# Long convolution with its matrices loaded and three tiles summed by taps; global attention in packed halves

## The chip, the core and the metric

The kernel runs on one core of a Trainium2 chip. Its time is the device time of one execution in microseconds (us). TensorE (PE, with PEld for its weight loads) multiplies into PSUM; VectorE (DVE), ScalarE (ACT) and GpSimd (POOL) work on SBUF and PSUM; SyncE (SP) and ScalarE issue DMAs.

## The reference

A network of two blocks, batch 1, 512 positions, width 1024, all float32. The first block has two layers, each a mixer (global attention, pooling, neighbourhood attention, gates) and a gated MLP with a convolution of 3 taps. The second has a conformer module, a convolution FFN, dilated attention and another FFN. The change touches two parts:

```python
def global_axial_attention(q, k, v, gq, gk):      # both layers: 8 query heads, 2 key heads, 64 wide
    q = rope_2d(rmsnorm(q, gq)) * 64 ** -0.5; k = rope_2d(rmsnorm(k, gk))
    s = jnp.einsum('bqkgd,bskd->bkgqs', qi, k)
    p = jax.nn.softmax(s, axis=-1)
    return jnp.einsum('bkgqs,bskd->bqkgd', p, v)

def conformer_conv_module(h, w_in, b_in, dw, dw_b, ln_g, ln_b, w_out, b_out):   # once
    u = h @ w_in + b_in
    u = u[..., :1024] * jax.nn.sigmoid(u[..., 1024:])
    u = causal_dwconv(u, dw, dw_b)                # 31 taps, each channel by itself
    u = jax.nn.silu(layer_norm(u, ln_g, ln_b))
    return u @ w_out + b_out
```

## The kernel before

Weights come as units of eight 128x128 tiles, 512 KB, in the order in which they are used: SP loads one (`raw`, 3 buffers), ACT rounds it to a high half (L295), DVE subtracts for the low half (L296), 4 buffers `w`. A product in float32 accuracy is three matmuls into one PSUM bank, high by high, high by low, low by high (`mm3`, L325 to L327). Activations stand transposed, features on partitions, 512 positions along the free side.

Every engine takes its instructions in an order fixed when the program is built. The stages are Python generators, called lanes: a lane yields an estimate of how long its next step has to wait, every matmul adds its estimate to a common clock (`spend`), and lanes that are due are written out between the matmuls of the main loop (`tick`). A scheduler then orders the instructions under the limits of the buffers.

**Global attention** (`axial_inputs`, `axial_lane`). Two query heads share the 128 partitions of a tile `qh`/`ql` (the pair is i, the head in it e). The keys of head e stand in 64 partitions of `kh`/`kl` [:, e], with zeros in the other 64, so scores for 128 queries are three 512-column matmuls (L862 to L864). After softmax (DVE maximum, ACT exponential, POOL scaling) the probabilities are transposed and split into `ph`/`pl`, and for each of four key blocks three 256-column matmuls (L890, L893, L894) add into `po`; values `vh`/`vl` carry zeros for the other head, and `po` of a pair collects four units. Two lanes run beside the gate and branch matmuls of `branch`.

**Long convolution** (`conv_inputs`). For each of 8 feature tiles j two projections are computed, ACT evacuates them (`ca` L1234, `cgs` L1239) and DVE multiplies them into `cu` with positions split by their remainder mod 4 (L1241). Sixteen small DMAs (L1249) bring that into `cup`, where a partition is a pair of remainder and channel. POOL builds matrices `cw` from the taps (L1224), and 36 plain float32 matmuls of 128 columns a tile do the 31 taps (L1264; the profile shows each as two records). DVE adds the bias (`vc`, L1274), PE transposes (`ctp`, L1281), ACT copies to `vt`, DVE takes statistics (L1288). When all eight tiles are in, statistics are joined (L1291), `vt` is normalised, and PE transposes it back (`ltp`, L1185) for the closing product. The first six projections (tiles 0 to 2) come out of the head, which runs while the norm of the stage ahead is still coming in.

Of the kernel before, what the change touches and what calls it, by code (L numbers as in the profile page):

```python
# [21 lines left out]
F32 = mybir.dt.float32  # L22
# [6 lines left out]
P = 128  # L29
# [14 lines left out]
CONV_M, CONV_PAD = 9, 8  # L44
AX_LANES, AX_SOFTMAX, AX_NEXT, AX_PROB = 2, 5.5, 2.0, 1.7
# [111 lines left out]
_vec("cm_b_in", 16)  # L157
for _n in ("cm_ln_g", "cm_ln_b", "kv_norm_g"):
    _vec(_n, 8)
# [11 lines left out]
def constants():  # L171
# [29 lines left out]
    c["same"] = np.tile(np.eye(32, dtype=np.float32), (4, 1))  # L201
# [25 lines left out]
class Kernel:  # L227
# [534 lines left out]
    def axial_inputs(self, l):  # L762
# [64 lines left out]
        return jobs, (kh, kl, vh, vl, qh, ql, rq), done  # L827
# [21 lines left out]
    def axial_lane(self, units, st, tiles, y):  # L849

        nc = self.nc
        kh, kl, vh, vl, qh, ql, rq = tiles
        yh, yl = y
        while units:
            i, u, e = units.popleft()
# [3 lines left out]
            for t in (2 * u, 2 * u + 1):  # L859
                cols = slice(t * P, (t + 1) * P)  # L860
                ps = self.psum("a", "sc")
                nc.tensor.matmul(ps, qh[:, i, cols], kh[:, e], start=True, stop=False)  # L862
                nc.tensor.matmul(ps, qh[:, i, cols], kl[:, e], start=False, stop=False)
                nc.tensor.matmul(ps, ql[:, i, cols], kh[:, e], start=False, stop=True)  # L864
                self.spend(0.65)
# [15 lines left out]
            if i not in st:  # L881
                st[i] = self.psum("b", "po")
                st[i, "n"] = 0
            po = st[i]
            cols = slice(2 * u * P, (2 * u + 2) * P)
            for k in range(4):
# [8 lines left out]
            self.spend(1.3)  # L895
            st[i, "n"] += 1
            if st[i, "n"] == 4:
                self.split_out(yh[:, i], yl[:, i], po)
# [303 lines left out]
    def conv_inputs(self):  # L1202

        nc, cv = self.nc, self.cv
        taps = cv.tile([P, 32, CONV_M, 4], F32, tag="taps", name="taps")
        nc.sync.dma_start(
            taps, self.t["cm_taps"].rearrange("p (g m q) -> p g m q", m=CONV_M, q=4)
        )  # L1210
        same = cv.tile([P, 32], F32, tag="same", name="same")
        nc.sync.dma_start(same, self.t["same"])
# [5 lines left out]
        held, phased, mats = [], {}, {}  # L1218
# [34 lines left out]

        def conv():
            for j in range(KD):
# [17 lines left out]
                vc = cv.tile([P, 4, P], F32, tag="vc", name="vc", bufs=2)  # L1273
# [37 lines left out]
        matrices(0)  # L1311
        matrices(1)
# [286 lines left out]
def arrange(inputs):  # L1599
# [44 lines left out]
    put("cm_b_in", a["cm_b_in_2"][0])  # L1644

# [3 lines left out]
    got["cm_taps"] = np.ascontiguousarray(  # L1649
# [32 lines left out]
```

## Time and profile before

| | us |
|---|---|
| median of 3 runs (3252.04 to 3722.86) | 3252.92 |
| the profiled execution | 3250.97 |
| its span, first to last instruction | 3249.2 |
| PE busy in it | 3157.3 |
| DVE busy in it | 1783.0 |
| ACT busy in it | 1329.3 |
| POOL busy in it | 493.7 |

The profile is of one execution. A matmul's record is longer than the time it takes from its neighbours, since matmuls overlap: what one costs in a dense row is the distance from its start to the next one's. A bracket at the end of a line is the idle time ahead of the instruction and what ended it. PEclk is the granted TensorE clock as a share of full speed.

### The profile page before, as it was taken

How to read it: one execution, taken by the hardware profiler on the slowest of the kernel's cores; microseconds unless marked ns; L12 is line 12 of the kernel's file. 1: busy time of each engine (PE TensorE's matmuls, PEld its weight loads, DVE VectorE, ACT ScalarE, POOL GpSimd, SP SyncE). 2: the span in 40 equal slices, each digit the busy share in tenths (PEclk: the TensorE clock that was granted, in tenths of full speed). 3: DMA queues.
4: the chain of work that ended last, by engine and by line, in shares of the span. 5: the costliest groups of instructions: out<-in, count | busy, mean ns of one | idle time of the engine just before them, and what ended most of it. 6: DMA issues, size and time to landing. Idle time of an engine off the chain costs nothing.

```text
span 3249.2 us, 41363 instructions
## 1 busy us (share of the span) xinstructions
PE 3157.3 (97%) x16172; PEld 2664.2 (82%) x16172; DVE 1783.0 (55%) x3187; ACT 1329.3 (41%) x2160; POOL 493.7 (15%) x448
## 2 busy tenths in 40 slices
PE   8999999999999999999999989999899999999998
PEld 7887888888888788888879868888788888888886
DVE  6668446456675753645465356446634454464555
ACT  5456334334444643434343154334333333353332
POOL 0113110000111322000005410000433334100001
PEclk9999999999999999999999989999999999999999
DMA  3112232222221222232232222222222222222221
GB/s 141 59 61 74 98 111 79 97 100 94 91 69 53 77 87 101 84 104 96 95 108 77 67 80 71 98 97 104 84 72 79 77 78 79 79 85 98 97 98 72
DMA packets 86403, 281.80 MB, mean 87 GB/s; under 512 B 11584, under 2 KB 17984, under 8 KB 86208
## 3 DMA queue, kind: packets, MB, share of 16 engines
q1 hardware_dynamic: 85632, 278.10, 24.7%
q8 instruction: 128, 2.10, 0.3%
q10 hardware_dynamic: 576, 1.05, 0.1%
q14 instruction: 67, 0.55, 0.1%
HBM read 274.91 MB, written 2.10 MB: 85 GB/s over the span
## 4 chain that ended last, share of the span: by engine, by line
PE 87%; DVE 8%; ACT 4%; issue 1%; DMA 0%; POOL 0%; SPq 0%; DVEq 0%; ACTq 0%; POOLq 0%
PE mm L327 18%; PE mm L326 18%; PE mm L325 18%; PE mm L511 6%; PE mm L512 6%; PE mm L513 6%; PE conv L1264 2%; ACT junk L382 2%; PE z L327 1%; PE z L326 1%; PE z L325 1%; DVE w L296 1%; PE htp L444 1%; PE pt L875 1%; PE dpo L1398 1%
## 5 line engine op out<-in xcount | busy, mean ns | idle before, releaser
L325 PE MATMUL mm<-hh,w 128*128 128x512 f32 (+1 forms) x2720 | 1052.7, 387 | 0.0
L326 PE MATMUL mm<-hl,w 128*128 128x512 f32 (+1 forms) x2720 | 1035.2, 381 | 0.0
L327 PE MATMUL mm<-hh,w 128*128 128x512 f32 (+1 forms) x2720 | 1035.0, 381 | 0.0
L296 DVE TENSOR_TENSOR w<-raw,w 128x1024 fp32r<-128x1024 f32 x436 | 567.8, 1302 | 465.7 <-ACT w L295 461.0
L327 PEld LDWEIGHTS mm<-hh,w 128*128 128x128 f32 x2720 | 511.8, 188 | 96.5 <-issue 1.2
L326 PEld LDWEIGHTS mm<-hl,w 128*128 128x128 f32 x2720 | 512.6, 188 | 90.4 <-issue 2.4
L325 PEld LDWEIGHTS mm<-hh,w 128*128 128x128 f32 x2720 | 512.3, 188 | 90.2 <-issue 1.9
L295 ACT ACTIVATE w<-raw 128x1024 fp32r<-128x1024 f32 x436 | 459.0, 1053 | 247.7 <-PE mm L513 187.0
L403 POOL TENSOR_TENSOR y<-y,row 128x512 f32<-128x512 f32 x40 | 54.3, 1389 | 1311.1 <-ACT junk L382 1311.1
L625 DVE SCALAR_TENSOR_TENSOR cg<-mm,vecs,cg 128x511 f32<-128x511 f32 (+1 forms) x176 | 131.9, 749 | 212.8 <-ACT cg L618 209.9
L292 POOL TENSOR_TENSOR raw<-raw,vecs 128x1024 f32<-128x1024 f32 x72 | 145.5, 2021 | 562.2 <-DMA raw<-in_wall 558.2
L512 PE MATMUL mm<-w,ah 128*128 128x512 f32 x576 | 226.5, 393 | 0.0
L511 PE MATMUL mm<-w,ah 128*128 128x512 f32 x576 | 225.7, 392 | 0.0
L513 PE MATMUL mm<-w,al 128*128 128x512 f32 x576 | 225.7, 392 | 0.0
L625 DVE SCALAR_TENSOR_TENSOR cv<-mm,vecs,cv 128x511 f32<-128x511 f32 (+1 forms) x176 | 131.9, 750 | 100.2 <-ACT cv L618 97.3
L618 ACT ACTIVATE cg<-mm,vecs 128x512 f32<-128x512 f32 x88 | 68.7, 781 | 286.3 <-PE mm L327 286.1
L326 PE MATMUL mm<-hl,keep 128*128 128x256 f32 x512 | 143.4, 282 | 7.0 <-DVE hl L675 6.9
L327 PE MATMUL mm<-hh,keep 128*128 128x256 f32 x512 | 142.9, 281 | 0.1
L325 PE MATMUL mm<-hh,keep 128*128 128x256 f32 x512 | 142.1, 284 | 0.2 <-ACT hh L674 0.2
L511 PEld LDWEIGHTS mm<-w,ah 128*128 128x128 f32 x576 | 109.1, 189 | 23.5 <-issue 0.8
L513 PEld LDWEIGHTS mm<-w,al 128*128 128x128 f32 x576 | 109.1, 189 | 22.6
L512 PEld LDWEIGHTS mm<-w,ah 128*128 128x128 f32 x576 | 109.1, 189 | 22.4
(287 smaller groups left out, 4552.8 us busy)
## 6 DMA issues: line engine op xcount, KB each, us to landing
raw<-in_wall SPq DMA_DIRECT2D x500, 512.0 KB, 3.2
row<-in_rows SPq DMA_DIRECT2D x9, 512.0 KB, 4.1
x<-in_x SPq DMA_DIRECT2D x4, 512.0 KB, 6.1
bt<-in_rpb SPq DMA_DIRECT2D x16, 128.0 KB, 2.1
cup<-cu SPq DMA_DIRECT2D x128, 16.0 KB, 1.8
out<-x SPq DMA_DIRECT2D x4, 256.0 KB, 2.1
out<-x ACTq DMA_DIRECT2D x4, 256.0 KB, 2.1
taps<-in_cm_taps SPq DMA_DIRECT2D x1, 576.0 KB, 4.9
```

Source lines behind the costliest of these rows:

```text
L292: nc.gpsimd.tensor_tensor(rows, rows, g[:, k0 : k0 + n, None].to_broadcast(list(rows.shape)), op=OP.mult)
L295: nc.scalar.activation(hi, raw, AF.Copy)
L296: nc.vector.tensor_tensor(lo, raw, hi.bitcast(F32), op=OP.subtract)
L325: nc.tensor.matmul(ps, wh, xh, start=first and i == 0, stop=False, **check)
L326: nc.tensor.matmul(ps, wh, xl, start=False, stop=False, **check)
L327: nc.tensor.matmul(ps, wl, xh, start=False, stop=stop, **check)
L382: self.nc.scalar.activation(junk, x, AF.Square, accum_out=total)
L511: nc.tensor.matmul(ps, xh, wh, start=first, stop=False)
L512: nc.tensor.matmul(ps, xh, wl, start=False, stop=False)
L513: nc.tensor.matmul(ps, xl, wh, start=False, stop=last)
L618: nc.scalar.activation(o, ps, AF.Identity, scale=self.vec(taps + str(k0), f), bias=self.vec(cb, f))
L625: nc.vector.scalar_tensor_tensor(o[:, to], ps[:, of], self.vec(taps + str(k), f), o[:, to], op0=OP.mult, op1=OP.add,)
```

## The change

**Attention.** The tile `q` [:, i, e] now holds head e alone: its high half in the 64 partitions of that head and its low half in the other 64. Keys stand in both halves of `kh` and `kl`, so one matmul with `kh` gives high by high and low by high together, and scores take two matmuls. `v` is packed in the same way, so `po` has two parts in its two halves, added at the end by ACT and DVE, once for each head rather than each pair. The zero fills go, the units run head by head.

**Convolution.** The matrices `cw` are laid out in DRAM and loaded by DMAs that ACT issues, 590 KB each, four a tile. Feature tiles 0 to 2 don't go to the matrices: they stay in the order of positions with 30 zeros ahead, ACT does tap 0 and the bias, DVE does 30 multiply-adds (`scalar_tensor_tensor`), and PE transposes the result as before. The taps stand in `vecs`, which grows from 868 to 1124 columns.

```diff
+CONV_DVE, CONV_TAP = 3, 1.0
...
+_vec("cm_dw_b", 8)
+for _k in range(31):
+    _vec(f"cm_dw{_k}", 8)
...
-        vh = self.ap.tile([P, 4, 2, P], F32R, tag="vh", name="vh")
-        vl = self.ap.tile([P, 4, 2, P], F32R, tag="vl", name="vl")
-        qh = self.ap.tile([P, 4, S], F32R, tag="qh", name="qh")
-        ql = self.ap.tile([P, 4, S], F32R, tag="ql", name="ql")
+        v = self.ap.tile([P, 4, 2, P], F32R, tag="v", name="v")
+        q = self.ap.tile([P, 4, 2, S], F32R, tag="q", name="q")
...
-        zero = self.rp.tile([P, S], F32, tag="wide", name="zero")
-        nc.gpsimd.memset(zero, 0.0)
-        none = zero[:, :256].rearrange("p (i d) -> p i d", i=4)
-        for v in (vh, vl):
-            nc.scalar.activation(v[:, :, 0, 64:], none, AF.Copy)
-            nc.scalar.activation(v[:, :, 1, :64], none, AF.Copy)
-        for k in (kh, kl):
-            nc.scalar.activation(k[64:, 0], zero[64:], AF.Copy)
-            nc.scalar.activation(k[:64, 1], zero[:64], AF.Copy)
...
-            for e, r in ((0, slice(0, 64)), (1, slice(64, P))):
+            for e in range(2):
+                r, o = ends[e], ends[1 - e]
                 nc.scalar.activation(kh[r, e], qg[r], AF.Copy)
-                nc.vector.tensor_tensor(kl[r, e], qg[r], kh[r, e].bitcast(F32), op=OP.subtract)
+                nc.scalar.activation(kh[o, e], qg[r], AF.Copy)
+                for to in (r, o):
+                    nc.vector.tensor_tensor(kl[to, e], qg[r], kh[r, e].bitcast(F32), op=OP.subtract)
...
-            self.split_out(vh[:, :, 0, :64], vl[:, :, 0, :64], pt[:, :, :64])
-            self.split_out(vh[:, :, 1, 64:], vl[:, :, 1, 64:], pt[:, :, 64:])
+            self.split_out(v[:, :, 0, :64], v[:, :, 0, 64:], pt[:, :, :64])
+            self.split_out(v[:, :, 1, 64:], v[:, :, 1, :64], pt[:, :, 64:])
...
-            self.split_out(qh[:, i], ql[:, i], qg)
+            for e in range(2):
+                r, o = ends[e], ends[1 - e]
+                nc.scalar.activation(q[r, i, e], qg[r], AF.Copy)
+                nc.vector.tensor_tensor(q[o, i, e], qg[r], q[r, i, e].bitcast(F32), op=OP.subtract)
...
-                nc.tensor.matmul(ps, qh[:, i, cols], kh[:, e], start=True, stop=False)
-                nc.tensor.matmul(ps, qh[:, i, cols], kl[:, e], start=False, stop=False)
-                nc.tensor.matmul(ps, ql[:, i, cols], kh[:, e], start=False, stop=True)
+                nc.tensor.matmul(ps, q[:, i, e, cols], kh[:, e], start=True, stop=False)
+                nc.tensor.matmul(ps, q[:, i, e, cols], kl[:, e], start=False, stop=True)
...
-                    po[:, cols], vh[:, k, e], a, start=st[i, "n"] == 0 and k == 0, stop=False, **check
-                )
-                nc.tensor.matmul(po[:, cols], vh[:, k, e], b, start=False, stop=False, **check)
-                nc.tensor.matmul(po[:, cols], vl[:, k, e], a, start=False, stop=k == 3, **check)
+                    po[:, cols], v[:, k, e], a, start=st[i, e, "n"] == 0 and k == 0, stop=False, **check
+                )
+                nc.tensor.matmul(po[:, cols], v[:, k, e], b, start=False, stop=k == 3, **check)
...
-                self.split_out(yh[:, i], yl[:, i], po)
+                r, o = (slice(0, 64), slice(64, P)) if e == 0 else (slice(64, P), slice(0, 64))
+                t = self.xp.tile([P, S], F32, tag="pot", name="pot", bufs=2)
+                nc.scalar.activation(t[r], po[o], AF.Copy)
+                nc.vector.tensor_tensor(t[r], t[r], po[r], op=OP.add)
+                self.split_out(yh[r, i], yl[r, i], t[r])
...
-                    units = deque((i, u, e) for i in range(4) for u in range(2) for e in range(2))
+                    units = deque((i, e, u) for i in range(4) for e in range(2) for u in range(2))
...
             w = self.cf.tile([P, 4, CONV_M, 4, 32], F32, tag="cw", name="cw", bufs=2)
             for i in range(4):
-                nc.gpsimd.tensor_tensor(
-                    w[:, i],
-                    taps[:, 4 * j + i, :, :, None].to_broadcast([P, CONV_M, 4, 32]),
-                    same[:, None, None, :].to_broadcast([P, CONV_M, 4, 32]),
-                    op=OP.mult,
+                nc.scalar.dma_start(
+                    w[:, i],
+                    self.t["cm_mats"][4 * (j - CONV_DVE) + i].rearrange(
+                        "p (m a b) -> p m a b", m=CONV_M, b=32
+                    ),
                 )
...
+            if j < CONV_DVE:
+                u = cv.tile([P, 30 + S], F32, tag="cw30", name="cw30", bufs=2)
+                nc.gpsimd.memset(u[:, :30], 0.0)
+                nc.vector.tensor_tensor(u[:, 30:], held.pop(), g, op=OP.mult)
+                plain[j] = u
+                return
...
+        def tap_sums():
+            for j in range(CONV_DVE):
+                while j not in plain:
+                    yield 0.5
+                yield 1.4
+                acc = cv.tile([P, S], F32, tag="cacc", name="cacc", bufs=2)
+                nc.scalar.activation(
+                    acc, plain[j][:, :S], AF.Identity, scale=self.vec("cm_dw0", j),
+                    bias=self.vec("cm_dw_b", j),
+                )
+                vc = cv.tile([P, 4, P], F32, tag="vc", name="vc", bufs=3)
+                for k in range(1, 31):
+                    yield CONV_TAP
+                    to, u, of = acc, plain[j][:, k : k + S], acc
+                    if k == 30:
+                        to = vc.rearrange("p q s -> p s q")
+                        u, of = (a.rearrange("p (s q) -> p s q", q=4) for a in (u, acc))
+                    nc.vector.scalar_tensor_tensor(
+                        to, u, self.vec(f"cm_dw{k}", j), of, op0=OP.mult, op1=OP.add
+                    )
...
         def conv():
-            for j in range(KD):
+            for j in range(CONV_DVE, KD):
...
+            while len(summed) < CONV_DVE:
+                yield 0.3
...
-        matrices(0)
-        matrices(1)
+        matrices(CONV_DVE)
+        matrices(CONV_DVE + 1)
+        self.spawn(tap_sums())
         self.spawn(conv())
```

Two places of the order that every engine follows are shown. The first is DVE's queue at the start of the convolution, from the first gated tile on: `w_` are low halves of weights, `cacc<-cw_14415` and `cacc<-cw_14422` taps of tile 0 and tile 1, `cu` and `vc` as above. Before:

```order
L1241 TENSOR_TENSOR cu<-ca,cgs 128x128x4 x2
L296 TENSOR_TENSOR w_14750<-raw_14608,w_14750 128x1024
L296 TENSOR_TENSOR w_14802<-raw_14748,w_14802 128x1024
L1241 TENSOR_TENSOR cu<-ca,cgs 128x128x4
L1274 TENSOR_TENSOR vc<-conv,cbias 128x512
```

And now:

```order
L1243 TENSOR_TENSOR cw_14415<-ca,cgs 128x512
L1243 TENSOR_TENSOR cw_14422<-ca,cgs 128x512
L1279 SCALAR_TENSOR_TENSOR cacc<-cw_14415,vecs,cacc 128x512 x2
L300 TENSOR_TENSOR w_14472<-raw_14433,w_14472 128x1024
L1279 SCALAR_TENSOR_TENSOR cacc<-cw_14415,vecs,cacc 128x512
L300 TENSOR_TENSOR w_14528<-raw_14470,w_14528 128x1024
L1279 SCALAR_TENSOR_TENSOR cacc<-cw_14415,vecs,cacc 128x512
L1279 SCALAR_TENSOR_TENSOR cacc<-cw_14422,vecs,cacc 128x512
L1279 SCALAR_TENSOR_TENSOR cacc<-cw_14415,vecs,cacc 128x512
L300 TENSOR_TENSOR w_14564<-raw_14526,w_14564 128x1024
```

The weights' low halves now stand between taps, and the taps of tiles 0 and 1 alternate; those of tile 2 come later, one behind the other, when tile 0 has given its buffer back. PE, which before went to the convolution of tile 0 after 7 matmuls of the fourth tile's projection, now does 99 matmuls first, and then the matrices of tile 3.

The second place is DVE's queue at the end of the convolution, up to the joining of the statistics (BN_AGGR). Before:

```order
L296 TENSOR_TENSOR w_15598<-raw_15552,w_15598 128x1024
L1274 TENSOR_TENSOR vc<-conv,cbias 128x512
L1288 BN_STATS stats<-ctp 128x6 x4
L1274 TENSOR_TENSOR vc<-conv,cbias 128x512
L1288 BN_STATS stats<-ctp 128x6 x4
L1291 BN_AGGR lmv<-stats 128x2 x4
```

And now:

```order
L300 TENSOR_TENSOR w_15390<-raw_15344,w_15390 128x1024
L1279 SCALAR_TENSOR_TENSOR cacc<-cw_14429,vecs,cacc 128x512 x6
L1313 TENSOR_TENSOR vc<-conv,cbias 128x512
L1327 BN_STATS stats<-ctp 128x6 x4
L1313 TENSOR_TENSOR vc<-conv,cbias 128x512
L1279 SCALAR_TENSOR_TENSOR vc<-cw_14422,vecs,cacc 128x128x4
L1279 SCALAR_TENSOR_TENSOR vc<-cw_14429,vecs,cacc 128x128x4
L1327 BN_STATS stats<-ctp 128x6 x4
L1290 BN_STATS stats<-ctp 128x6 x8
L1332 BN_AGGR lmv<-stats 128x2 x4
```

The last taps of tiles 1 and 2 stand behind the bias of the last matrix tile, and eight more statistics follow.

## Rows read from the trace of the kernel before

**Rows 1.** The page, part 1: busy us of each engine, share, instructions.

```profile
PE 3157.3 (97%) x16172; PEld 2664.2 (82%) x16172; DVE 1783.0 (55%) x3187; ACT 1329.3 (41%) x2160; POOL 493.7 (15%) x448
```

**Rows 2.** The page, part 4: the chain that ended last, by engine.

```profile
PE 87%; DVE 8%; ACT 4%; issue 1%; DMA 0%; POOL 0%; SPq 0%; DVEq 0%; ACTq 0%; POOLq 0%
```

**Rows 3.** Busy us by stretch: PE, PEld, DVE, ACT, POOL, PEclk, DMA share, GB/s.

```profile
50.00:90.00 40.00, 39.45 (x196) 30.30 (x195) 34.97 (x96) 20.65 (x33) 6.33 (x4) 1.00 0.23 80
91.00:223.00 132.00, 130.96 (x726) 111.55 (x725) 76.87 (x165) 63.62 (x122) 24.37 (x33) 1.00 0.15 53
1752.70:1877.50 124.80, 123.20 (x850) 112.55 (x848) 43.62 (x54) 22.18 (x29) 67.07 (x35) 1.00 0.21 67
1877.50:1893.60 16.10, 4.82 (x21) 3.67 (x21) 10.43 (x28) 11.17 (x12) 0.00 (x0) 0.55 0.41 130
```

**Rows 4.** PE's timeline in layer 0's attention: start us, us, engine, line, operation.

```profile
109.41 0.39 PE L864 MATMUL sc<-kh,ql 128*128 128x512 f32 x1
109.64 0.28 PE L890 MATMUL po<-ph,vh 128*128 128x256 f32 x1
...
109.99 0.28 PE L890 MATMUL po<-ph,vh 128*128 128x256 f32 x1
```

**Rows 5.** Groups by line, both layers: count | busy us, mean ns | idle before.

```profile
L894 PE MATMUL po<-ph,vl 128*128 128x256 f32 x128 | 36.1, 282 | 0.0
L864 PE MATMUL sc<-kh,ql 128*128 128x512 f32 x64 | 25.2, 394 | 0.0
...
L1050 DVE TENSOR_TENSOR wot<-wot,wpo 64x512 f32<-64x512 f32 x16 | 11.0, 686 | 6.7 <-ACT wot L1049 6.2
```

**Rows 6.** PE's timeline: the third score of layer 0.

```profile
94.61 0.50 PE L862 MATMUL sc<-kh,qh 128*128 128x512 f32 x1 [0.88 <-DVE rrs L757]
```

**Rows 7.** PE's timeline at the end of the convolution.

```profile
1867.83 8.20 PE L1264 MATMUL conv<-cup,cw 128*128 128x128 f32 x72
1876.82 0.66 PE L1281 MATMUL ctp<-ident,vc 128*128 128x128 f32 x4 [0.78 <-DVE vc L1274]
1886.61 2.98 PE L1185 MATMUL ltp<-ident,vt 128*128 128x128 f32 x12 [9.13 <-DVE vt L1306]
...
1894.57 0.63 PE L511 MATMUL mm<-w,ch 128*128 128x512 f32 x1
1895.00 0.63 PE L512 MATMUL mm<-w,ch 128*128 128x512 f32 x1
```

**Rows 8.** DVE's timeline in an FFN: dependent multiply-adds, then a weight's low half.

```profile
575.25 1.54 DVE L625 SCALAR_TENSOR_TENSOR cg<-mm,vecs,cg 128x511 f32<-128x511 f32 x2 [2.77 <-ACT cg L618]
576.70 1.22 DVE L296 TENSOR_TENSOR w<-raw,w 128x1024 fp32r<-128x1024 f32 x1
577.83 0.69 DVE L642 TENSOR_TENSOR cg<-cg,cv 128x512 f32<-128x512 f32 x1
```

**Rows 9.** DVE's timeline near the end: independent multiply-adds from SBUF.

```profile
3243.23 2.74 DVE L409 SCALAR_TENSOR_TENSOR x<-y,rst,x 128x512 f32<-128x512 f32 x4
```

**Rows 10.** DVE's timeline in the convolution.

```profile
1859.33 1.07 DVE L1241 TENSOR_TENSOR cu<-ca,cgs 128x512 f32<-128x512 f32 x1 [1.89 <-ACT cgs L1239]
...
1876.07 0.69 DVE L1274 TENSOR_TENSOR vc<-conv,cbias 128x512 f32<-128x512 f32 x1 [6.52 <-PE conv L1264]
1878.14 0.89 DVE L1288 BATCH_NORM_STATS2 stats<-ctp 128x6 f32<-128x128 f32 x4 [1.38 <-ACT vt L1284]
1878.95 1.04 DVE L1291 BATCH_NORM_AGGREGATE lmv<-stats 128x2 f32<-128x48 f32 x4
```

**Rows 11.** ACT's timeline: the gate of tile 2.

```profile
1752.94 0.69 ACT L1239 ACTIVATE cgs<-mm,vecs 128x512 f32<-128x512 f32 x1 [1.30 <-PE mm L327]
```

**Rows 12.** SP's queue: the sixteen DMAs of one tile.

```profile
1860.56 10.01 SPq L1249 DMA_DIRECT2D cup<-cu  x16
```

**Rows 13.** DMA issues by tile: KB each, median us to landing.

```profile
raw<-in_wall SPq DMA_DIRECT2D x500, 512.0 KB, 3.2
```

**Rows 14.** DVE's timeline at the start.

```profile
7.76 0.26 DVE L1550 TENSOR_SCALAR hb<-vecs 128x24 f32<-128x24 f32 x2 [6.89 <-DMA vecs<-in_vecs]
```

More of the change, by code (lines that the diff above doesn't have):

```diff
@@ L200, in constants @@
     c["nmask"] = np.stack([edge, inside], 1).astype(np.float32)
-    c["same"] = np.tile(np.eye(32, dtype=np.float32), (4, 1))
     q = np.arange(P)[:, None]
@@ L766, in axial_inputs @@
         kl = self.ap.tile([P, 2, S], F32R, tag="kl", name="kl")
-        vh = self.ap.tile([P, 4, 2, P], F32R, tag="vh", name="vh")
-        vl = self.ap.tile([P, 4, 2, P], F32R, tag="vl", name="vl")
-        qh = self.ap.tile([P, 4, S], F32R, tag="qh", name="qh")
-        ql = self.ap.tile([P, 4, S], F32R, tag="ql", name="ql")
+        v = self.ap.tile([P, 4, 2, P], F32R, tag="v", name="v")
+        q = self.ap.tile([P, 4, 2, S], F32R, tag="q", name="q")
         rq = self.ap.tile([P, 4, 8], F32, tag="rq", name="rq")
-        zero = self.rp.tile([P, S], F32, tag="wide", name="zero")
-        nc.gpsimd.memset(zero, 0.0)
-        none = zero[:, :256].rearrange("p (i d) -> p i d", i=4)
-        for v in (vh, vl):
-            nc.scalar.activation(v[:, :, 0, 64:], none, AF.Copy)
-            nc.scalar.activation(v[:, :, 1, :64], none, AF.Copy)
-        for k in (kh, kl):
-            nc.scalar.activation(k[64:, 0], zero[64:], AF.Copy)
-            nc.scalar.activation(k[:64, 1], zero[:64], AF.Copy)
+        ends = (slice(0, 64), slice(64, P))
         done = [False] * 4
@@ L826, in axial_inputs @@
             jobs.append((gemm_tiles("w_in", l, [T_Q + i], range(KD)), lambda ps, i=i: on_q(ps, i)))
-        return jobs, (kh, kl, vh, vl, qh, ql, rq), done
+        return jobs, (kh, kl, v, q, rq), done
     def softmax_rows(self, ps, scale_col, scale, pmat, mx=None):
@@ L851, in axial_lane @@
         nc = self.nc
-        kh, kl, vh, vl, qh, ql, rq = tiles
+        kh, kl, v, q, rq = tiles
         yh, yl = y
         while units:
-            i, u, e = units.popleft()
+            i, e, u = units.popleft()
             while not st["ready"][i]:
@@ L880, in axial_lane @@
                 yield AX_PROB
[L881 to L884, printed above, removed]
+            if (i, e) not in st:
+                st[i, e] = self.psum("b", "po")
+                st[i, e, "n"] = 0
+            po = st[i, e]
             cols = slice(2 * u * P, (2 * u + 2) * P)
@@ L890, in axial_lane @@
                 nc.tensor.matmul(
-                    po[:, cols], vh[:, k, e], a, start=st[i, "n"] == 0 and k == 0, stop=False, **check
+                    po[:, cols], v[:, k, e], a, start=st[i, e, "n"] == 0 and k == 0, stop=False, **check
                 )
-                nc.tensor.matmul(po[:, cols], vh[:, k, e], b, start=False, stop=False, **check)
-                nc.tensor.matmul(po[:, cols], vl[:, k, e], a, start=False, stop=k == 3, **check)
-            self.spend(1.3)
-            st[i, "n"] += 1
-            if st[i, "n"] == 4:
-                self.split_out(yh[:, i], yl[:, i], po)
+                nc.tensor.matmul(po[:, cols], v[:, k, e], b, start=False, stop=k == 3, **check)
+            self.spend(0.95)
+            st[i, e, "n"] += 1
+            if st[i, e, "n"] == 2:
+                r, o = (slice(0, 64), slice(64, P)) if e == 0 else (slice(64, P), slice(0, 64))
[3 more added lines that the diff above has]
+                self.split_out(yh[r, i], yl[r, i], t[r])
     def window_inputs(self, l):
@@ L1206, in conv_inputs @@
         nc, cv = self.nc, self.cv
-        taps = cv.tile([P, 32, CONV_M, 4], F32, tag="taps", name="taps")
-        nc.sync.dma_start(
-            taps, self.t["cm_taps"].rearrange("p (g m q) -> p g m q", m=CONV_M, q=4)
-        )
-        same = cv.tile([P, 32], F32, tag="same", name="same")
-        nc.sync.dma_start(same, self.t["same"])
         bias = cv.tile([P, 32], F32, tag="cbias", name="cbias")
@@ L1217, in conv_inputs @@
         stats = cv.tile([P, 4, KD, 6], F32, tag="stats", name="stats")
-        held, phased, mats = [], {}, {}
+        held, phased, mats, plain = [], {}, {}, {}
         def matrices(j):
@@ L1252, in on_g @@
             phased[j] = up
+        summed = []
+        def tap_sums():
[18 more added lines that the diff above has]
+                    )
+                yield 1.0
+                pt = self.psum("a", "ctp")
+                for q in range(4):
+                    nc.tensor.transpose(pt[:, q * P : (q + 1) * P], vc[:, q], self.ident)
+                self.spend(0.45)
+                by = pt.rearrange("s (q c) -> s q c", q=4)
+                nc.scalar.activation(vt[:, :, j * P : (j + 1) * P], by, AF.Copy)
+                for q in range(4):
+                    nc.vector.bn_stats(stats[:, q, j], by[:, q])
+                summed.append(j)
         def conv():
-            for j in range(KD):
+            for j in range(CONV_DVE, KD):
                 while min(j + 1, KD - 1) not in phased:
@@ L1272, in conv @@
                     matrices(j + 2)
-                vc = cv.tile([P, 4, P], F32, tag="vc", name="vc", bufs=2)
+                vc = cv.tile([P, 4, P], F32, tag="vc", name="vc", bufs=3)
                 nc.vector.tensor_tensor(
@@ L1644, in arrange @@
     put("cm_b_in", a["cm_b_in_2"][0])
+    put("cm_dw_b", a["cm_dw_b_2"][0])
+    for k in range(31):
+        put(f"cm_dw{k}", a["cm_dw_2"][0, k])
     dw = np.pad(a["cm_dw_2"][0][::-1], ((3, 6), (0, 0))).reshape(40, 32, 32)
     q, m, p = np.ogrid[:4, :CONV_M, :4]
-    got["cm_taps"] = np.ascontiguousarray(
-        dw[4 * m + p - q + 3].transpose(0, 4, 3, 1, 2).reshape(P, 32 * CONV_M * 4)
-    )
+    taps = dw[4 * m + p - q + 3].transpose(0, 4, 3, 1, 2)[:, :, 4 * CONV_DVE :]
+    mats = np.zeros((taps.shape[2], 4, 32, CONV_M, 4, 32), np.float32)
+    for c in range(32):
+        mats[:, :, c, :, :, c] = taps[:, c].transpose(1, 0, 2, 3)
+    got["cm_mats"] = mats.reshape(-1, P, CONV_M * P)
     got["cm_dw_b"] = np.ascontiguousarray(np.tile(a["cm_dw_b_2"][0].reshape(32, 32).T, (4, 1)))
```

2 lines of the change are left out of this document (1 added, 1 removed).

## The prediction, made before the changed kernel ran

> **What bounds the kernel now.** I began with the page: PE is busy for 97% of the span, DVE for 55%, ACT for 41% [rows 1]. The chain of waits says the same of the end: 87% of it is PE, 8% DVE, 4% ACT, and DMA rounds to nothing [rows 2]. So a PE instruction that goes is a gain unless something else of its stage takes its place, and I read each stage by stretches, since the averages hide the tight ones [rows 3]. While the attention is set up (50 to 90 us) PE is busy 39.45 of 40 us, but DVE 34.97 too, so there is little room on DVE. In layer 0's attention itself (91 to 223) it is 130.96 of 132 against 76.87. In the conformer's projections and convolution (1752.7 to 1877.5) it is 123.20 of 124.8, with DVE at 43.62, ACT at 22.18, and POOL at 67.07 for the matrices. Behind that lie 16.1 us in which PE does 4.82 us of work at a granted clock of 0.55.
>
> **Attention: what PE loses.** Records overlap, so the price is the distance between starts: a 512-column matmul in a dense row takes 109.64 − 109.41 = 0.23 us, three of 256 columns take 0.35, so one takes 0.117 [rows 4]. Both layers together lose 64 of the first kind and 128 of the second [rows 5]: 64 × 0.23 + 128 × 0.117 = 14.7 + 15.0 = 29.7 us.
>
> **Attention: what DVE and ACT get.** A DVE operation on 64 partitions and 512 columns takes 0.69 us [rows 5]. Setting up, kl takes 4 such instead of 2, and each of four pairs takes two for q's low half instead of one of the whole height. That is 6 × 0.69 = 4.1 us a layer, where DVE has 5 of 40 us free. About five of them, 3.4 us, stand ahead of the third score, which waits 0.88 us for DVE already [rows 6]. By the order of the new kernel, five more gate matmuls (1.1 us) come in front of that score and two score matmuls fewer (0.46), so some 0.6 of it is covered. DVE's own free time takes in part of the other 2.8; I take 1.8 us a layer as lost, between 0 and 3.4. The zero fills that go were ACT's and POOL's, which nobody waited for: nothing. The sum of two halves (an ACT copy, a DVE addition, eight splits on 64 partitions instead of four on 128) adds about twelve operations a layer to DVE and as many to ACT, 8 us each beside 132 us in which DVE has 55 free: hidden. If that cover goes, at most the last head's own chain of four (2.8 us) stands at the end. For that, and because softmax now has about 11% less PE work beside it, I take 1.0 us a layer, between 0 and 4. Attention nets 29.7 − 2 × 2.8 = **24.1 us**; the ends are 29.7 and 29.7 − 2 × 7.4 = 14.9.
>
> **Convolution: what PE loses.** A tile's 36 matmuls take 8.20 us [rows 7]; three tiles go: 24.6 us. Left in the stage are 240 projection matmuls × 0.227 = 54.5, five tiles × 8.2 = 41.0 and transposes for 3.6. PE could end at 1752.7 + 99.1 = 1851.8.
>
> **Convolution: what DVE gets.** 90 multiply-adds on 128x512. No row shows such a chain on SBUF alone. The nearest rows bound it: two dependent ones of an FFN take 1.54 with the next beginning at 576.70, so about 0.79 apart once the record of the last is taken off [rows 8]; four independent ones take 2.74, which is 0.66 apart with 0.75 for the last [rows 9]. In the new order about 60 alternate between two tiles or have a weight's low half between them, and 30 (of tile 2, mostly) follow each other. I take 60 × 0.66 + 30 × 0.79 = 63.3, plus 3 × 0.4 = 1.2 for the three last taps, whose output is strided as cu's is (1.07 against 0.69 [rows 10]). The rest of the queue: 12 low halves × 1.13 [rows 8] = 13.6; five cu (1.07), five vc (0.69) and eight groups of statistics (0.85 to 0.89) [rows 10], and two plain products, make 15.6. Together 93.7. The first tap can start once ACT has made the gate (1752.94 for tile 2 [rows 11]) and tap 0: about 1754.4. DVE so ends at 1848, 4 us ahead of PE: near a tie, and DVE's work is not evenly spread. When a matrix tile's bias must wait behind taps, its transposes wait too (0.78 already [rows 7]); I take 2.0 us for these stalls. At the end, the joining of the statistics came 2.9 us after the last convolution matmul (1876.03 to 1878.95 [rows 7, 10]). Now two strided taps (2 × 1.1) and eight more statistics stand between, part of them beside PE's end: 5.5, so 2.6 more.
>
> The matrices come by DMA, 20 loads of 590 KB behind ACT. 512 KB land in 3.2 us [rows 13] and the order issues each tile's set a convolution ahead, so I cost the loads at nothing; their issues on ACT, a few tenths each, hide in an engine with 100 of 125 us free. POOL's 67 us go, and nobody waited for them. The sixteen small DMAs on SP still take 10.0 us a tile [rows 12], against 13.7 for one projection pair and 8.2 for one convolution: they stay hidden. The 9.13 us gap behind the stage [rows 7] is a chain of normalisation that isn't touched: it moves, whole. Net **24.6 − 2.0 − 2.6 = 20.0 us**; with all stalls hidden 24.6, with the bounds of the tap price below.
>
> **Start.** `vecs` grows by 256 columns, 131 KB, and DVE's first operation waits for it until 7.76 us [rows 14]. At the rate of [rows 13] that is 0.8 us; 0.4 to 1: **0.7 lost**.
>
> **Sum.** 24.1 + 20.0 − 0.7 = 43.4 us off the profiled execution's 3250.97, which lies 1.95 below the median of the runs shown: 3207.6, or **3208**. That is 1.3%. About 2% (65 us) is what a measurement of this kernel can tell from no change, and even with nothing lost, 54.3 us, the change stays inside it.
>
> **Rivals.**
>
> *DVE bounds the convolution.* If every tap costs 0.79, DVE has 60 × 0.13 = 7.8 us more and ends at 1855.9, with the joining, the stalls and PE's last transposes behind it: the convolution saves 12 instead of 20, so 3215. For it: 94 us of DVE in a stage of 99. Against: the four operations at 0.66 apart [rows 9]. The chain's own taps must be 0.79 in any case. The Trainium skill ("VectorE: DVE Perf Modes", section "The DRAIN you can't avoid") says that an operation does not begin until the pipe of the one before is empty; by that alternation would buy nothing and this rival would hold, but the 0.66 of [rows 9] disagrees with that rule. Chance 0.22.
>
> *Everything hides.* DVE keeps ahead in both stages and stalls fall in slack: 29.7 + 24.6 − 0.7 = 53.6, 3197. For it: DVE is only half busy in the kernel. Chance 0.15.
>
> *Attention was not bound by PE alone.* With two score matmuls in place of three, lanes wait on their own softmax chains and the set-up loses its full 3.4 us. The stage then gives 12 instead of 24: 3220. Against: 130.96 of 132 us busy [rows 3] and the gate matmuls as filler. Chance 0.10.
>
> *Matrices late.* 11.8 MB more in a stage that now moves 67 GB/s × 124.8 us = 8.4 MB [rows 3]. At the 130 GB/s of the stretch behind [rows 3] 20.2 MB take 155 us, 30 more than the stage has now: the saving of 20 turns into a loss of 30, and with 24.1 for attention the time is about 3258, slower than before by 0.2%. It decides if the DMA engines cannot pass some 200 GB/s. Against: their share there was 0.41 [rows 3], and 512 KB in 3.2 us is 160 GB/s for a single one [rows 13]. Chance 0.05, most of it for partial lateness, 3230 to 3245.
>
> *Slower by the clock.* PE idles behind DVE, again and again, for the bias or the low halves that now stand between taps, and the granted clock falls to 1.2 GHz in the stage. After the 9.13 us gap that is what rows show: 0.55 granted [rows 3] and matmuls 0.43 apart instead of 0.23 [rows 7]. If half the stage's 99 us ran so, it would cost 50 us: 3258; nearly all, the 88 us behind the first projections, 3296. It decides once the stalls come in rows of several us. The Trainium skill ("TensorE: Matmul & The Clock Gate", section "HAM oscillation — how this bites in real kernels") describes a kernel whose every gap drops the clock again; the 0.55 behind the gap agrees. Against: in my sum the stalls are under a microsecond each. Chance 0.03.
>
> **Numbers.** The forecast, 3200 to 3213, has 0.45; then 0.22, 0.15, 0.10, 0.05, 0.03. The range goes from the rival in which everything hides to just beyond the two DVE rivals: 3195 to 3226; outside lie the late matrices, the clock and the bad ends of both stages together. Faster by over 2% needs more than PE loses in all: 0.03. Slower by over 2% needs 65 us, of which only the clock comes near: 0.01. Within 2%: 0.96.
>
> **What would show it.** In the new profile: the statistics joined about 18 to 21 us earlier from the first gate on; taps about 0.66 apart where they alternate and 0.79 where they follow each other; DVE busy for some 95 of the stage's 100 us; a longer wait of PE for vc than 0.78; a third score that waits 2 to 3 us for DVE in place of 0.88; attention about 24 us shorter over both layers; POOL some 70 us less busy; DVE's first operation at about 8.4. The prediction is wrong if a tap's price lies outside 0.66 to 0.79, if convolution matmuls wait for matrices, if the granted clock falls below 1.00 ahead of the joining, or if the attention's gaps grow past 3 us a layer.

## The result, and the profile after

The changed kernel takes 3213.51 us (median of 4 runs, 3209.82 to 3215.70) against 3252.48 for the kernel before: a ratio of 0.9881, interval 0.9862 to 0.9901, 39 us or 1.2%. One of the four runs of the kernel before took 3722.86 us and is left out of the ratio. The forecast was 3208 in a range of 3195 to 3226. The profiled execution, at 3215.7 us, is the longest of the four; its span is 3213.9, 35.3 less than the 3249.2 before.

The page, part 1, answers to [rows 1]:

```profile
PE 3114.8 (97%) x15764; PEld 2617.7 (81%) x15764; DVE 1853.6 (58%) x3310; ACT 1349.2 (42%) x2183; POOL 423.2 (13%) x414
```

PE is still the bound. It is busy 42.5 us less, DVE 70.6 more, POOL 70.5 less. The stretches that answer to [rows 3], in the same columns (set-up of the attention; attention; convolution; the gap behind it):

```profile
54.00:94.00 40.00, 39.84 (x198) 30.86 (x197) 35.16 (x91) 19.72 (x30) 6.37 (x4) 1.00 0.22 72
96.00:215.00 119.00, 116.95 (x627) 96.59 (x626) 85.39 (x183) 72.51 (x134) 24.56 (x33) 1.00 0.18 58
1729.50:1834.40 104.90, 102.27 (x658) 91.38 (x656) 90.35 (x138) 25.60 (x34) 0.37 (x3) 1.00 0.42 141
1834.40:1850.50 16.10, 5.11 (x22) 3.94 (x22) 11.38 (x33) 11.45 (x12) 0.00 (x0) 0.50 0.41 131
```

PE stays full beside a DVE that is now busy for 90 of 105 us in the convolution, and the granted clock there is 1.00 throughout. Where the 35 us of these two profiles come from is read by cutting both traces at the same PE instructions, the transposes that begin each stage (`htp`, and `ltp` behind the convolution). Differences of their start times, in us:

| | before | after | difference |
|---|---|---|---|
| start, to the last transposes ahead of layer 0's attention | 32.1 | 35.8 | +3.7 |
| layer 0, attention to the transposes of its FFN | 450.4 | 438.4 | −12.0 |
| layer 1, the same | 446.2 | 435.6 | −10.6 |
| from the conformer's first transposes to `ltp` | 185.4 | 161.1 | −24.3 |
| from `ltp` to the end: nothing changed there | 1362.6 | 1370.7 | +8.1 |

The two FFNs between differ by 0.3. So the changed stages gave 47, and 12 were lost at the start and behind.

DVE's taps, where those of two tiles alternate (first row), where those of tile 2 follow each other (second), and at the end of the stage, which answers to [rows 10]:

```profile
1764.69 6.72 DVE L1279 SCALAR_TENSOR_TENSOR cacc<-cw,vecs,cacc 128x512 f32<-128x512 f32 x10
...
1803.19 7.83 DVE L1279 SCALAR_TENSOR_TENSOR cacc<-cw,vecs,cacc 128x512 f32<-128x512 f32 x10
...
1821.49 0.68 DVE L1313 TENSOR_TENSOR vc<-conv,cbias 128x512 f32<-128x512 f32 x1
...
1830.96 0.69 DVE L1313 TENSOR_TENSOR vc<-conv,cbias 128x512 f32<-128x512 f32 x1 [6.52 <-PE conv L1303]
1831.57 2.04 DVE L1279 SCALAR_TENSOR_TENSOR vc<-cw,vecs,cacc 128x512 f32<-128x512 f32 x2
1833.46 0.87 DVE L1327 BATCH_NORM_STATS2 stats<-ctp 128x6 f32<-128x128 f32 x4
1834.24 1.73 DVE L1290 BATCH_NORM_STATS2 stats<-ctp 128x6 f32<-128x128 f32 x8
1835.89 1.04 DVE L1332 BATCH_NORM_AGGREGATE lmv<-stats 128x2 f32<-128x48 f32 x4
```

Less a last record of 0.73, ten alternating taps are 0.665 apart, ten chained ones 0.79. From 1822 on DVE has only the two strided last taps and statistics left, and waits 6.52 us for PE: it had done all the rest some 9 us ahead. PE there, answering to [rows 7]:

```profile
1822.72 8.20 PE L1303 MATMUL conv<-cup,cw 128*128 128x128 f32 x72
1831.71 0.66 PE L1320 MATMUL ctp<-ident,vc 128*128 128x128 f32 x4 [0.78 <-DVE vc L1313]
1832.82 0.63 PE L1285 MATMUL ctp<-ident,vc 128*128 128x128 f32 x4 [0.46 <-DVE vc L1279]
1833.76 0.66 PE L1285 MATMUL ctp<-ident,vc 128*128 128x128 f32 x4 [0.31 <-DVE vc L1279]
1843.23 2.98 PE L1190 MATMUL ltp<-ident,vt 128*128 128x128 f32 x12 [8.81 <-DVE vt L1347]
```

The bias comes 0.78 us behind the matmuls, as before; the last taps of two tiles and their statistics make the tail longer. The start of the third score, answering to [rows 6], and DVE's first operation, answering to [rows 14]:

```profile
100.28 0.50 PE L864 MATMUL sc<-kh,q 128*128 128x512 f32 x1 [1.42 <-DVE rrs L761]
```

```profile
9.59 0.26 DVE L1592 TENSOR_SCALAR hb<-vecs 128x24 f32<-128x24 f32 x2 [8.72 <-DMA vecs<-in_vecs]
```

The DMA issues (KB each, median us to landing; 576 KB are the 590 thousand bytes of a matrix load), answering to [rows 13], and a set of matrices on ACT's queue:

```profile
raw<-in_wall SPq DMA_DIRECT2D x500, 512.0 KB, 3.5
cw<-in_cm_mats ACTq DMA_DIRECT2D x20, 576.0 KB, 6.6
```

```profile
1763.09 5.72 ACTq L1224 DMA_DIRECT2D cw<-in_cm_mats  x4
1768.86 0.60 ACT L1323 ACTIVATE vt<-ctp 128x512 f32<-128x512 f32 x1 [12.79 <-PE mm L331]
```

The four issues stretch over 5.7 us, and `vt` stands behind them. The row merges them: the first is over at 1763.44, and in a view from 1764 on the other three stand by themselves:

```profile
1767.48 1.33 ACTq L1224 DMA_DIRECT2D cw<-in_cm_mats  x3
```

So an issue takes some 0.4 us here, and between the first and the second ACT's queue stands for 4.0, until a semaphore that, as far as the trace can tell, came with SP's DMAs into `cup`. PE waits neither for the matrices nor for this `vt`.

### The profile page after: what moved, and what is told of

It reads as the page before. It is cut to its first block, busy times and chain, and to the rows that moved or that the text cites. A ratio compares the mean times of both kernels' runs of the same rounds, so it can differ in the third digit from the quotient of the medians.

```text
span 3213.9 us, 40538 instructions
## 1 busy us (share of the span) xinstructions
PE 3114.8 (97%) x15764; PEld 2617.7 (81%) x15764; DVE 1853.6 (58%) x3310; ACT 1349.2 (42%) x2183; POOL 423.2 (13%) x414
## 4 chain that ended last, share of the span: by engine, by line
PE 82%; DVE 10%; ACT 4%; issue 2%; DMA 1%; SPq 1%; POOL 0%; ACTq 0%; DVEq 0%; POOLq 0%
PE mm L331 18%; PE mm L330 18%; PE mm L329 18%; PE mm L515 6%; PE mm L517 6%; PE mm L516 6%; ACT junk L386 2%; DVE w L300 2%; PE z L329 1%; PE z L331 1%; PE z L330 1%; PE htp L448 1%; DVE cacc L1279 1%; PE pt L876 1%; PE dpo L1440 1%
```

## The experiments

All times are medians beside runs of the kernel before on the same chip.

**attn_only and conv_only: each part alone.** The first is the kernel before with the attention's part of the diff, the second with the rest.

> The kernel before with the attention's part of the change alone. My theory: the attention is bound by PE and loses 64 matmuls of 512 and 128 of 256 columns, worth 29.7 us, and gives back a few us to DVE while it is set up; in the changed kernel the two stages gained some 24 us. So 3252 - 24 = 3228, the first DVE operation back at 7.8 us, and nothing lost behind the last attention. Rival (lanes wait on their own softmax): under 15 us gained, 3238 or more. Second rival (the stage gains more when nothing else is changed): 3222.

> The kernel before with the long convolution's part alone (matrices loaded, three tiles by taps, vecs of 1124 columns). Theory: the stage itself gains about 22 us as in the changed kernel, the start loses about 3 us to the larger vecs, so 3252 - 19 = 3233 if nothing is given back later, and 3238 if the 6 to 8 us that the changed kernel gives back in stages behind the convolution belong to the convolution's change. Rival: the two parts help one another, then this gains under 12 us (3240 or more).

Measured: 3234.53 (ratio 0.9943, 0.9928 to 0.9958) and 3233.24 (0.9938, 0.9923 to 0.9953) against 3253.59. The stages gain what they gain together: layers 0 and 1 take 438.8 and 434.6 in attn_only, the convolution 162.2 in conv_only. But attn_only gains 19 us where 24 were expected, and its trace shows most of why: from `ltp` on, behind a convolution that it doesn't touch, it needs 1367.5 instead of 1362.6 (1364.4 in before_again, below). conv_only needs 1368.0 there, though its time is the 3233 expected if nothing were lost behind: the 3 us that it was to lose at the start didn't come. So the loss behind belongs to neither part in particular.

**after_again and before_again: both kernels once more.**

> The changed kernel, nothing edited. Theory: 3213, and its profile again loses some 3 us at the start and 4 to 8 us in the unchanged stages behind the convolution against the kernel before. Rival: the loss behind the convolution is of that one execution, then this profile shows under 3 us of it and a span near 3208.

> The kernel before, nothing edited, for a second profile. Theory: the 7 to 8 us by which the stages behind the convolution are longer in every profile since belong to those executions and not to the change: their 512 KB loads take 3.5 to 3.7 us at the median against 3.2 in the first profile. So this profile too shows loads of about 3.5 us and some 1367 to 1370 us from the first transposes behind the convolution to the end, where the first had 1362.6. Rival: the change lengthens those stages; then this shows 1362 to 1364 again.

Measured: after_again 3214.03, ratio 0.9879 (0.9864 to 0.9894), span of the profile 3210.9; 1369.5 from `ltp` on. before_again 3253.11; 1364.4 from `ltp` on, loads of 3.3 us:

```profile
raw<-in_wall SPq DMA_DIRECT2D x500, 512.0 KB, 3.3
```

My theory for before_again falls: the 5 to 8 us do come with the changed programs, and don't scatter from execution to execution. Over all fourteen profiles, the three of programs with loads of 3.2 to 3.3 us have 1362.5 to 1364.4, the eleven with 3.4 us or more have 1367.5 to 1372.9. The loss doesn't grow with the landing time: attn_only and conv_only have loads of 3.7, the latest, and the smallest losses of the changed programs.

**vecs_wide: only the larger constants.**

```diff
 _vec("cm_b_in", 16)
+_vec("cm_dw_b", 8)
+for _k in range(31):
+    _vec(f"cm_dw{_k}", 8)
```

> The kernel before with nothing but vecs at 1124 columns instead of 868 (the taps lie in it and nobody reads them). Theory: two things that the changed kernel shows come without any of its work. DVE's first operation moves from 7.7 to about 8.5 us, and the 512 KB loads take 3.5 us or more at the median, where the kernel before shows 3.2 and 3.3, so that the stages behind the convolution take 1367 us or more instead of 1362.6 to 1364.4: some 3256 in all. Rival: loads and stages stay as in the kernel before (3.2 to 3.3 us, 1362 to 1365), then the changed work itself lengthens them.

Measured: one run of 3252.03; 1362.5 from `ltp` on, loads of 3.3 us, so this one profile shows no slower loads with the larger tile. DVE's first operation:

```profile
9.37 0.26 DVE L1553 TENSOR_SCALAR hb<-vecs 128x24 f32<-128x24 f32 x2 [8.50 <-DMA vecs<-in_vecs]
```

**split: the taps in a tile of their own, loaded later.**

```diff
+        tapv = cv.tile([P, 32, KD], F32, tag="tapv", name="tapv")
+        nc.sync.dma_start(tapv, self.t["cm_tapv"].rearrange("p (k j) -> p k j", j=KD))
...
-                        to, u, self.vec(f"cm_dw{k}", j), of, op0=OP.mult, op1=OP.add
+                        to, u, tapv[:, k, j : j + 1], of, op0=OP.mult, op1=OP.add
```

> The changed kernel with the taps and their bias in a tile of their own, loaded on SP when the convolution begins, so that vecs is back at its 868 columns less none. Theory: the start's loss comes from the 131 KB more in vecs, so the first DVE operation is back at 7.8 us instead of 9.6 and PE's first transposes at 11.5 instead of 13.3, worth 2 to 3 us: 3210.5. Rival: the later start of the one profile was chance, then DVE's first operation stays anywhere between 7.8 and 9.6 and the time at 3213. A tap's price stays 0.66 and 0.79.

Measured: 3211.76, ratio 0.9872 (0.9855 to 0.9888), not to be told from after_again. Its first operation missed the expected 7.8 us:

```profile
8.56 0.26 DVE L1591 TENSOR_SCALAR hb<-vecs 128x24 f32<-128x24 f32 x2 [7.69 <-DMA vecs<-in_vecs]
```

With 868 columns the profiles show 7.64 to 7.94, and this 8.56; with 1124, in nine profiles, 8.1 to 9.6. On the mean the first operation comes 0.7 us later with 1124 columns (8.65 against 7.92), with a scatter larger than that. At the last transposes ahead of layer 0's attention the means are 33.8 and 33.3.

**late2: loads that land later, in the kernel before.**

```diff
-            self.nc.sync.dma_start(raw, self.t["wall"][u].rearrange("p (i m) -> p i m", m=P))
+            wall = self.t["wall"][u].rearrange("p (i m) -> p i m", m=P)
+            for a, b in ((0, 2), (2, 8)):
+                self.nc.sync.dma_start(raw[:, a:b], wall[:, a:b])
```

> The kernel before with each 512 KB load in two DMAs, of 128 and 384 KB, so that the larger part is issued about 0.4 us later and the unit is complete some 0.2 to 0.4 us later. Theory: the dilated stage is sensitive to when loads land, because POOL scales weights on landing and collides there with DVE, so its 441 us become 444 to 445 and the stages behind the convolution 1366 or more: 3256. Rival: PE is never short of weights and the loads' landing is hidden, nothing changes: 3252.5.

Measured: 3258.92, ratio 1.0019 (1.0010 to 1.0029). A unit is now complete 3.5 us after its first issue, and from `ltp` on the kernel needs 1368.9. The dilated stage (dilated attention), from the first scores to the last transposes, in the kernel before, the changed kernel and late2 (columns as in [rows 3]):

```profile
2385.50:2826.10 440.60, 438.63 (x2256) 368.22 (x2255) 212.34 (x511) 147.48 (x286) 157.20 (x129) 1.00 0.22 78
```

```profile
2346.80:2790.90 444.10, 439.72 (x2257) 367.91 (x2256) 217.97 (x511) 147.46 (x286) 159.39 (x129) 1.00 0.23 77
```

```profile
2390.60:2836.90 446.30, 439.76 (x2265) 368.36 (x2263) 219.83 (x506) 145.96 (x285) 156.25 (x129) 1.00 0.23 76
```

DVE is busy for 5.6 and 7.5 us longer with the same work. What PE waits for there (us in total, times, longest), again before, after and late2; `dw` are weights by which DVE joins two softmax results and PE's `dwb` spreads them, `dsm` probabilities that POOL has scaled and PE transposes into `dpt`:

```profile
PE dwb L358 <- DVE dw L1450: 2.0, 6, 0.4
```

```profile
PE dwb L362 <- DVE dw L1492: 3.3, 6, 0.6
PE dpt L1428 <- POOL dsm L1422: 0.9, 3, 0.3
```

```profile
PE dwb L360 <- DVE dw L1452: 4.5, 6, 1.1
PE dpt L1388 <- POOL dsm L1382: 2.1, 5, 0.5
```

POOL scales most of this stage's units of weights as they land (58 scalings beside 64 low halves on DVE). What that does to a low half, in the changed kernel, when POOL has begun first and when DVE has:

```profile
2415.58 1.90 POOL L296 TENSOR_TENSOR raw<-raw,vecs 128x1024 f32<-128x1024 f32 x1 [2.61 <-DMA raw<-in_wall]
2415.85 2.71 DVE L300 TENSOR_TENSOR w<-raw,w 128x1024 fp32r<-128x1024 f32 x1 [0.93 <-ACT w L299]
```

```profile
2404.14 1.23 DVE L300 TENSOR_TENSOR w<-raw,w 128x1024 fp32r<-128x1024 f32 x1 [3.05 <-ACT w L299]
2404.71 2.41 POOL L296 TENSOR_TENSOR raw<-raw,vecs 128x1024 f32<-128x1024 f32 x1 [4.71 <-DMA raw<-in_wall]
```

In the first pair DVE's record ends 1.08 us behind POOL's, in the second POOL's ends 1.75 behind DVE's: these two operations don't run at the same time, and the one that comes second waits. It is so throughout this stage: in each profile 18 to 21 of the 64 low halves begin beside a scaling under way, and every one ends 1.08 us behind it, whenever it began; the others take 1.2 us. What these low halves take over 1.23 us sums to 17.4 to 18.7 us in the three profiles with loads of 3.2 to 3.3 us, and to 21.5 to 24.9 in the eleven others: as many wait, but behind scalings that began later. PE's waits in the stage are 2.0 to 2.7 us in the three, 3.8 to 6.5 in the others. So late2 makes the kernel before show the changed kernel's loss in this stage. It also doubles the issues on SP; halves, below, does that too, and its stage is no longer than early's (444.0 and 445.0).

**dve0, dve2, dve4: none, two or four tiles by taps instead of three.** One constant; dve4 needs four buffers for the plain tiles and three for the sums.

```diff
-CONV_DVE, CONV_TAP = 3, 1.0
+CONV_DVE, CONV_TAP = 2, 1.0
```

> The changed kernel with no tile by taps: all eight by matrices, 32 loads of 590 KB (18.9 MB). Theory: loads cost nothing, POOL's work was off the path, so the stage takes the 184 to 185 us of the kernel before from the first transposes ahead of it to those behind, and the time is that of the attention's part alone with 1 us for the start: 3235. Rival (matrices late): convolution matmuls wait on their loads, 3245 or more.

> The changed kernel with two tiles by taps instead of three, so one more by matrices. Theory (PE sets the stage's end, DVE has some 9 us in hand): PE has 8.2 us more, the tail behind the last convolution matmul is one group of statistics and one tap shorter, so 3213.5 + 7 = 3220.5. Rival (DVE bounds the stage with three tiles): the time stays or falls, 3206 to 3214.

> The changed kernel with four tiles by taps and, so that it can be scheduled, 4 buffers for the plain tiles and 3 for the sums. PE loses 8.2 us more, DVE gets 30 taps more (some 20 us) less two operations of the matrices' way. Theory (with three tiles DVE has some 9 us in hand, with four it lacks some 10): DVE ends after PE, PE idles in the stage's end, 3213.5 + 8 = 3222, more (up to 3235) if the granted clock falls meanwhile. Rival (PE still the bound): 3205.

Measured: dve0 3237.76 (0.9954, 0.9939 to 0.9969), dve2 3224.08 (0.9916, 0.9902 to 0.9931), dve4 3224.55 (0.9914, 0.9899 to 0.9929; its four runs scatter from 3217.20 to 3227.78). All three are 2.5 to 3.6 us above what was expected. From the conformer's transposes to `ltp` they take 186.6, 171.5 and 172.1 us, the changed kernel 161.1 and 162.2. The stage as it was takes 183.8 to 185.8 in the five profiles that have it. So loading instead of building costs 1 to 3 us in one profile, of which 1.83 are a wait of PE for `cup` that the others don't have; the first two tiles that go to DVE give 7.5 each, the third 9 to 10 (in dve2 PE waits 2.1 us once for `vc`, where the changed kernel waits 1.1), and the fourth costs 10 to 11. In dve4 the last convolution matmuls are over at 1824, and PE waits for taps:

```profile
1826.03 0.63 PE L1285 MATMUL ctp<-ident,vc 128*128 128x128 f32 x4 [0.46 <-DVE vc L1279]
1830.69 1.09 PE L1285 MATMUL ctp<-ident,vc 128*128 128x128 f32 x4 [4.03 <-DVE vc L1279]
1843.18 1.09 PE L1285 MATMUL ctp<-ident,vc 128*128 128x128 f32 x4 [11.40 <-DVE vc L1279]
1853.07 2.98 PE L1190 MATMUL ltp<-ident,vt 128*128 128x128 f32 x12 [8.81 <-DVE vt L1347]
```

This is the rival in which DVE bounds the stage, one tile further on. Its clock in the same place:

```profile
1830.00:1846.00 16.00, 2.18 (x8) 1.43 (x8) 13.89 (x24) 2.30 (x4) 0.00 (x0) 0.51 0.30 98
```

From the end of the wait of 4.03 us PE is granted 1.2 GHz. The Trainium skill ("TensorE: Matmul & The Clock Gate", section "HAM oscillation — how this bites in real kernels") describes a kernel whose matmuls start at the lower clock again behind each of its waits; this 0.51 agrees. In the changed kernel no wait of PE between the first tap and the joining is over 1.1 us, and the clock stays at 1.00 until the stage's last transposes.

**early: the last taps ahead of the last bias.**

```diff
-CONV_DVE, CONV_TAP = 3, 1.0
+CONV_DVE, CONV_TAP = 3, 0.6
...
-                vc = cv.tile([P, 4, P], F32, tag="vc", name="vc", bufs=3)
+                vc = cv.tile([P, 4, P], F32, tag="vcp", name="vcp", bufs=3)
                 for k in range(1, 31):
```

> The changed kernel with the results of the taps in buffers of their own (vcp, 3) and 0.6 us instead of 1.0 as the taps' estimate, which puts the last taps of tiles 1 and 2 and the transposes and statistics of tile 1 ahead of the bias of the last matrix tile. Theory: the 1.7 us that the end of the stage is longer than before come from two strided taps of 1.0 and the statistics behind that bias, so the time from the last convolution matmul to the first transposes behind falls from 12.5 to about 10: 3211. Rival: the chain behind is bound by ACT's loads of weights and the copies, then nothing changes: 3213.5.

Measured: 3211.49, ratio 0.9878 (0.9862 to 0.9895): by time not told from the changed kernel. The trace shows the edit do about half of what was expected: from the last convolution matmul to `ltp` 11.3 us instead of 12.5.

```profile
1828.85 0.66 PE L1320 MATMUL ctp<-ident,vc 128*128 128x128 f32 x4 [0.79 <-DVE vc L1313]
1829.34 0.60 PE L1285 MATMUL ctp<-ident,vcp 128*128 128x128 f32 x4
1839.10 2.98 PE L1190 MATMUL ltp<-ident,vt 128*128 128x128 f32 x12 [9.16 <-DVE vt L1347]
```

**halves: early, with each load in two of 256 KB.** The edit is that of late2 with `((0, 4), (4, 8))`.

> The changed kernel with the taps' results in buffers of their own and each 512 KB load cut in two DMAs of 256 KB. Theory: the halves land earlier than one load of 512 KB (3.5 us), near 3.0, so POOL's scaling in the dilated stage gets its old place beside DVE or a better one: its 445 us become 441 or less, the stages behind the convolution 1364 to 1367, the whole 3206. Rival: twice the issues on SP or smaller pieces land no earlier, 3211.5.

Measured: 3210.37, ratio 0.9869 (0.9852 to 0.9885). A miss: the pieces land 2.7 and 3.0 us after issue, but the second is issued 0.37 us behind the first, so a unit is complete after 3.36 instead of 3.5. The dilated stage stays at 444.0, the part behind `ltp` at 1370.3. The lowest median of all is not told from the changed kernel by its interval.

## Why the prediction came out right, point by point

**Attention, 24.1 forecast: 22.6 in the first profile, 23.1 in after_again.** The price per matmul and the count hold. Of 14.85 us a layer, the stretch from the first score to the last `po` gives 12.5 to 12.8, so 2.0 to 2.3 are lost there and not 1.0; setting up takes 1.4 us longer in layer 0 and 1.8 to 2.4 in layer 1, where 1.8 was taken. The third score waits 1.42 us for DVE, less than the 2 to 3 expected. The rival in which softmax binds falls.

**Convolution, 20.0 forecast: 24.3 against the first profile of before, 23.0 between the means of two each.** The tap's two prices were right to the hundredth: of 63 distances between neighbouring taps 33 are 0.66 and 30 are 0.77 to 0.80. Alternating taps begin 0.665 us apart beside a record of 0.73, so one begins before the record ahead of it ends. The Trainium skill ("VectorE: DVE Perf Modes", section "The DRAIN you can't avoid") says in the same paragraph as the rule that the prediction weighed that an operation that isn't held starts earlier; the alternating taps agree with that exception and not with the strict rule.

The 2.0 us for stalls were mis-sized: PE waits 2.6 us for `vc` in the stage where it waited 1.6, and 0.8 of the difference lie in the tail, so 0.3 are left for them. The tail was taken 2.6 longer and is 1.7 longer (12.58 from the last convolution matmul to `ltp`, 10.85 before). With these two 24.6 becomes 22.6. DVE waits 1.38 and 6.52 us ahead of the last bias, and 3.6 us of its work (two last taps, two groups of statistics) are held back behind it: some 4 in hand, as in the sum. dve2 and dve4 show that PE binds with two and three tiles, DVE with four. Matrices were not late. Their issues cost ACT a few tenths each, as taken; the 4 us for which its queue stands between two of them were hidden. The 13.7 us for one projection pair doesn't fit the prediction's own 54.5 for five, 10.9 each; the sixteen DMAs' 10.0 stay under that too.

**Start, 0.7 forecast: 0.7 on the mean of the profiles.** The 3.7 of the first pair is scatter for the most part: to the same transposes before_again takes 34.0 and after_again 33.2.

**The signs.** One sign of being wrong came by the letter: in the first profile the clock falls at 1834.2, 1.7 us ahead of the joining at 1835.89. PE was then at the last of the convolution's transposes, so it cost next to nothing ahead of the joining; in after_again it falls 0.1 us behind it. And by the number alone the rival in which DVE bounds the convolution, at 3215, is nearer to 3213.51 than the forecast, which lies just outside the 3200 to 3213 that had a chance of 0.45. The alternating taps' 0.665 and dve2 rule that rival out.

**The step that failed** is the one that priced all stages behind the convolution at nothing: "it moves, whole" was said of the gap, and the sum had no term for anything later. There the changed kernel loses 5 to 8 us without one changed instruction, 6.9 between the means of its two profiles and the three with early loads. Of these, 2.9 lie in the dilated stage (441.6 to 444.45), and late2 shows their mechanism: loads that land 0.3 us later shift POOL's scaling against DVE. The other 4.0 stand ahead of that stage, from `ltp` to the first scores (498.6 to 502.6), and go with the clock, as in the first 80 us of them, before and after:

```profile
1886.60:1966.60 80.00, 71.73 (x388) 60.35 (x388) 47.97 (x97) 42.43 (x72) 11.14 (x8) 0.94 0.22 76
```

```profile
1843.20:1923.20 80.00, 72.68 (x365) 61.21 (x366) 46.07 (x93) 40.99 (x69) 11.00 (x8) 0.89 0.23 76
```

0.94 and 0.89 mean some 10 and 18 us at the lower level. Up to the first scores it is 20 to 23 us in the three profiles with early loads and 26 to 35 in the eleven others, though PE's idle time there is no longer (22.3 to 23.5 us, and 21.4 to 23.0). late2's one profile has 26 there and takes 500.8, 2 of the 4 us; why the clock is lower in the rest was not shown. The sum came out near partly by luck, because its errors had opposite signs: 3 us too little from the convolution on one side, and on the other 1 too much from the attention and 5 to 8 of loss behind that were not in it.

**What stays open** is why loads take 3.4 us or more in the changed programs. It shows from the first eighth of the span on and in both parts alone (3.7 each), so it is neither the matrices' traffic nor DVE's taps; the one profile of vecs_wide speaks against the larger constants.

## What to carry to other kernels

On an engine that is 97% busy, matmuls taken away are worth at most their distance in a dense row, here 23 us of 29.7 and 23 of 24.6, as long as the engine that takes over stays a few us ahead; count how far ahead, since one more tile turned a gain of 9 to 10 us into a loss of 10 to 11. Interleave two accumulations where each step depends on the last: 0.665 us a step instead of 0.79. And when gains of 1% are summed, allow some us for stages that nobody touched: operations that landings release can come to stand worse to one another, and only a second profile of both kernels tells that from scatter.

## What was not expected of the hardware

The same 512 KB loads land after 3.2 to 3.3 us in the kernel before and in vecs_wide, and after 3.5 to 3.7 in attn_only, conv_only and the changed kernel, over the whole span. 0.3 us of it, put in by hand with twice as many issues, cost 6 us in all (0.0019 × 3252), where the DMA engines were busy for 0.23 of the dilated stage. And a DVE subtraction that begins while POOL scales a unit of weights doesn't slow down by a share: it ends 1.08 us behind POOL, about as if it had only then begun (1.2 us alone).
